# A two-layer mixture-of-experts transformer on one core: the first layer's experts in another order, the context kept on chip

## Chip, cores and metric

The kernel runs on one core of a Trainium2 chip, with fp32 inputs and outputs. The metric is the device time of one execution in microseconds, as the median of several runs. The profiler's record of one execution gives the durations and waits below; times inside it count from the start of its span.

## What is computed

512 latent tokens and 256 context tokens of width 1024 pass two layers. A layer is an attention block (three parallel head groups, one output projection) and a block of 16 experts in which each expert chooses its tokens. The second layer updates the latents alone. The change touches the expert block and the norm behind the last layer:

```python
def ec_ffn(h, router_w, w_gate, w_up, w_down):
    n_tok, d = h.shape[1], h.shape[2]
    cap = EC_CAPACITY_FACTOR * n_tok // N_EXPERTS     # 64 of 512 latents, 32 of 256 context tokens
    aff = jax.nn.softmax((h @ router_w).astype(jnp.float32), axis=-1)
    top_aff, idx = lax.top_k(jnp.swapaxes(aff, 1, 2), cap)
    xg = jax.vmap(lambda hb, ib: hb[ib])(h, idx)
    hid = jax.nn.silu(jnp.einsum('becd,edf->becf', xg, w_gate)) * jnp.einsum('becd,edf->becf', xg, w_up)
    y = jnp.einsum('becf,efd->becd', hid, w_down) * top_aff[..., None].astype(h.dtype)
    return jax.vmap(lambda yb, ib: jnp.zeros((n_tok, d), yb.dtype).at[ib.reshape(-1)].add(yb.reshape(-1, d)))(y, idx)
...
    xl = xl + g2 * ec_ffn(rmsnorm(xl, norm2_g) * (1 + sc2) + sh2, router_w, w_gate, w_up, w_down)
    if update_ctx:
        xc = xc + cg2 * ec_ffn(rmsnorm(xc, norm2_g) * (1 + csc2) + csh2, router_w, w_gate, w_up, w_down)
...
    return rmsnorm(xl, final_norm_g)
```

## The kernel before

**Streams and names.** `li` is the layer, `upd` is true in layer 0. Stream `r = 0` is the latents (four blocks of 128 tokens, `xl`), `r = 1` the context (two blocks, `xc`). Weights come from DRAM in slots of 1 MB; an expert has six (gate and up by `load_gu`, down by `load_d`, issued on SyncE's queue, `Q`). Layer 0 has 14 slots in its ring, layer 1 has 18. `S` is ScalarE (ACT), `V` VectorE (DVE), `G` GpSimd (POOL).

**Choice.** After the output projection (`wo_half`) each block is routed (`route_half`): its logits, its softmax `lg`, its normalised rows `xn` written to the DRAM table `tabx` by a DMA that GpSimd issues, and its part of `affT` (`place`, the third of the `steps`). `Choice.rounds` finds the largest entries of each expert, eight at a time, and `Choice.finish` merges two halves into the list `lt`, transposes it on TensorE and leaves the token numbers in `gidx` (rows 0 to 63 latents, 64 to 95 context).

**Experts.** `gather(e)` fetches an expert's rows from `tabx` into `xg`, which has one buffer, by an indirect DMA of GpSimd. `columns(e)` transposes them in eight TensorE operations through the PSUM tile `tp`; ACT (latents) and DVE (context) scale them into `xgT`. `gate_up(e, r)` multiplies them with the gate and up weights: latents in a tile 64 tokens wide with 512 columns, context in one 32 wide with 256. ACT takes the silu, DVE the product (`gh`). `hid_t(e, r)` transposes that and ACT copies it to `hTe`; `down(e, r)` multiplies with the down weights. In layer 1 two experts share one gather of 128 rows and one `columns`.

**Results.** In layer 0 the experts 0 to 11 (`in_dram = 12`) write `ya`, which an indirect DMA of GpSimd adds to rows of a DRAM table `acc` (one per stream); before, `acc` gets a copy of `xl` and `xc`, and later the sums are loaded back. The other experts stay on chip: the result is split into two parts of reduced mantissa (`yt`, `yp`; for four context experts together `split`, `yc`), a 0/1 matrix `pl` (`places`, on GpSimd) puts the rows back by matmuls into a PSUM tile `cb` with two buffers, and DVE adds `cb` to `xl` or `xc` half a block at a time (`combine`, a list `todo` of pieces; `fill(n)` issues n of them between other work).

**Order.** TensorE runs in the order in which the code is written. The other engines' orders come from a scheduler, before the run, and are fixed. The loop over experts is, in the order of TensorE (layer 0; layer 1 has no `r = 1`): `gate_up(e,0)`, `hid_t(e-1,·)`, some pieces, `columns(e+1)`, `gate_up(e,1)`, some pieces, `down(e-1,·)`. The reload of `xl` and `xc` from `acc` is issued on GpSimd at expert 13, ahead of the last gather in GpSimd's queue.

Of the kernel before, what the change touches and what calls it, by code (L numbers as in the profile page):

```python
# [9 lines left out]
F32 = mybir.dt.float32  # L10
# [9 lines left out]
D = 1024  # L20
# [24 lines left out]
def hybrid_kernel(ctx: ExitStack, tc: tile.TileContext, a, out):  # L45
# [108 lines left out]
    accs = [dram.tile([n, D], F32, name=f"acc{n}") for n in (NL, NCX)]  # L154
# [85 lines left out]
    def layer(li, ada):  # L240
# [535 lines left out]

        es_r = ExitStack()
# [11 lines left out]
        for r, grp in enumerate(streams):  # L789
            t = rt.tile([48, len(grp) * 64], F32, name=f"affT{r}")  # L790
            G.memset(t, 0.0)
            aff.append(t)
# [8 lines left out]
        def split_wo(hf, blk):  # L801
            o = [wop.tile([128, 512], F32R, name=f"wo{j}") for j in range(2)]
            parts(wraw[hf, blk // 4][:, blk % 4], o, S.copy)
            wo[blk] = o

        def wo_half(tb, hf, before=None, after=None, fill=()):
# [3 lines left out]
            for blk in range(8):  # L810
# [3 lines left out]
                wa, wb = wo[blk]  # L814
# [16 lines left out]
        def route_half(tb, hf):  # L831
# [12 lines left out]
            def logits():  # L844
# [19 lines left out]
                if upd:  # L864
                    i = tb - CB if tb >= CB else tb
                    G.dma_start(accs[r][i * 128:(i + 1) * 128, :], x)
# [17 lines left out]
        class Choice:  # L884


            def __init__(self, r):
                self.r, self.c = r, 0
                self.val = rt.tile([48, caps[r]], F32, name=f"val{r}")
                self.idx = rt.tile([48, caps[r]], U32, name=f"idx{r}")  # L890
                self.a = [aff[r], rt.tile([48, 4 * caps[r]], F32, name=f"affb{r}")]
# [15 lines left out]
            def finish(self):  # L907
                r, cap, np_ = self.r, caps[self.r], nparts[self.r]
                rows = 128 // np_
                v0, v1 = self.val[0:NE], rt.tile([NE, cap], F32, name="mgv")  # L910
                V.tensor_copy(v1, self.val[32:48, ::-1])
                lt = rt.tile([NE, 2, 128], F32, name="lt")
                i0, i1, ge = [rt.tile([NE, cap], F32, name=f"mg{i}") for i in range(3)]
# [30 lines left out]
                if upd:  # L944
# [12 lines left out]
        if not upd:  # L957
            load_gu(1)
        steps = []
        for hf in range(2):  # L960
            for n, tb in enumerate(tbs):
                last = n == len(tbs) - 1
                wo_half(tb, hf, (lambda blk: split_wo(0, blk)) if hf + n == 0 else None,
                        (lambda blk: split_wo(1, blk)) if hf == 0 and last else None, steps)
                steps = route_half(tb, hf)
                if hf and tb < CB:
# [16 lines left out]
        es_r.close()  # L983

# [14 lines left out]
        xgs, xgTs = {}, {}  # L999

        def gather(e):
# [306 lines left out]
```

## Time and profile before

| | |
|---|---|
| median of three runs | 1456.85 us (1455.22 to 1459.57) |
| the profiled execution | 1453.06 us, span 1451.3 us |
| TensorE, matmul | 1280.1 us busy (88% of the span) |
| VectorE / ScalarE / GpSimd | 687.3 / 517.6 / 242.2 us busy |
| mean granted TensorE clock | 0.953 of full speed |
| DMA, whole run | 321.14 MB, mean 221 GB/s |
| first expert's first matmul, layer 0 / layer 1 | 524.13 / 1204.79 us |

The time is set by chains that pass from engine to engine. TensorE is busy in most of the span, so the places that matter are those where it waits, and the length of the repeated pieces. A granted clock of 1.00 is 2.4 GHz; stretches under it had TensorE at 1.2 GHz for a part.

### The profile page before, as it was taken

Reading aid. Unit: us, or ns where it says so; the run is one execution under the profiler, and the core shown is the slowest. Engines: PE = TensorE matmul, PEld = TensorE weight load, DVE = VectorE, ACT = ScalarE, POOL = GpSimd, SP = SyncE. Lnnn points to the kernel's source line nnn. Section 1 sums busy time; section 2 is a strip of 40 time slices with the busy share of each in tenths; the row PEclk is TensorE's granted clock in tenths of the full one; section 3 lists DMA queues with packets and bytes.
Section 4 is the critical chain, followed back from the end, with each engine's and each line's share of the span. In section 5 each row is a group of like instructions: output and inputs, shape, how many; then the busy total and the mean of one; then the engine's idle time right before and its main releaser. Section 6 shows DMA issues by size and latency. Waiting matters only on the chain. (4 is left out here: it accounts for less than half of the span.)

```text
span 1451.3 us, 21505 instructions
## 1 busy us (share of the span) xinstructions
PE 1280.1 (88%) x8542; PEld 800.0 (55%) x8542; DVE 687.3 (47%) x1516; ACT 517.6 (36%) x1095; POOL 242.2 (17%) x266
## 2 busy tenths in 40 slices
PE   3989989999999869999996969998999958999994
PEld 0768866666678624444443438876777843343331
DVE  1545356566743632222222474847776351333435
ACT  2523145455533322222222143436666322232222
POOL 1111001212210222222221020102232011111203
PEclk9989999999999979999998969999999978999998
DMA  8523315444732489999999310110012857999991
GB/s 355 187 99 116 149 63 215 175 182 182 291 145 82 190 314 361 367 373 370 373 371 399 133 56 32 71 62 1 1 41 70 341 222 308 419 418 420 419 416 62
DMA packets 56195, 321.14 MB, mean 221 GB/s; under 512 B 8720, under 2 KB 10384, under 8 KB 22560
## 3 DMA queue, kind: packets, MB, share of 16 engines
q1 hardware_dynamic: 45664, 286.75, 50.7%
q0 software_dynamic: 10432, 33.04, 7.3%
q8 instruction: 67, 1.10, 0.3%
q14 instruction: 32, 0.26, 0.1%
HBM read 304.52 MB, written 15.24 MB: 220 GB/s over the span
## 5 line engine op out<-in xcount | busy, mean ns | idle before, releaser
L59 PE MATMUL mm<-slot,xgT 128*64 128x512 f32 (+1 forms) x2048 | 290.6, 493 | 0.8 <-DMA slot<-in_exp_w_up_dram 0.7
L59 PE MATMUL mm<-hT,w 128*128 128x512 f32 (+1 forms) x1176 | 230.8, 356 | 3.0 <-POOL w L140 2.0
L59 PEld LDWEIGHTS mm<-hT,w 128*128 128x128 f32 x1176 | 192.6, 192 | 37.5 <-POOL w L140 2.4
L59 PEld LDWEIGHTS mm<-slot,xgT 128*64 128x64 f32 (+1 forms) x2048 | 104.8, 125 | 170.5 <-issue 143.8
L59 PE MATMUL mm<-slot,hTe 128*32 128x256 f32 (+1 forms) x1024 | 146.8, 490 | 0.8 <-ACT hTe L1057 0.8
L1048 DVE TENSOR_TENSOR gh<-mm,gh 64x512 f32<-64x512 f32 (+1 forms) x48 | 29.0, 604 | 218.4 <-ACT gh L1047 218.4
L1047 ACT ACTIVATE gh<-mm 64x512 f32<-64x512 f32 (+1 forms) x48 | 24.9, 518 | 278.1 <-PE tp L1055 171.8
L59 PE MATMUL mm<-wo,mixb 128*128 128x512 f32 x360 | 98.2, 409 | 2.3 <-DVE mixb L140 1.4
L59 PEld LDWEIGHTS mm<-slot,hTe 128*32 128x32 f32 (+1 forms) x1024 | 48.9, 123 | 88.7 <-issue 71.3
L694 ACT COPY pt<-tp 128x512 f32<-128x512 f32 (+1 forms) x120 | 64.9, 542 | 81.3 <-PE tp L691 80.2
L691 PE MATMUL tp<-ident,p 128*128 128x128 f32 x552 | 87.1, 283 | 5.5 <-ACT pt L694 2.3
L1023 ACT ACTIVATE xgT<-tp,modT,a 128x64 f32<-128x64 f32 (+1 forms) x192 | 70.1, 425 | 58.7 <-PE tp L1019 54.3
L681 POOL TENSOR_SCALAR p<-p,sm 128x768 f32<-128x768 f32 (+1 forms) x30 | 58.5, 1951 | 124.3 <-DVE sm L680 116.0
L691 PEld LDWEIGHTS tp<-ident,p 128*128 128x128 f32 x552 | 61.1, 142 | 27.1 <-issue 18.0
L59 PEld LDWEIGHTS mm<-wo,mixb 128*128 128x128 f32 x360 | 65.1, 191 | 16.2 <-DVE mixb L140 2.2
L59 PE MATMUL ada<-slot,sT 128*32 128x512 f32 x384 | 53.7, 678 | 22.9 <-DMA slot<-in_ada_w_dram 22.9
L59 PE MATMUL sc<-kt,qh 96*128 96x512 f32 (+1 forms) x324 | 69.7, 348 | 0.0
L139 ACT CAST w<-slot 128x1024 fp32r<-128x1024 f32 x30 | 31.4, 1046 | 100.1 <-PE mm L59 73.8
L59 PE MATMUL sc<-kst,qst 128*128 128x256 f32 (+1 forms) x288 | 48.2, 298 | 20.5 <-DVE mx L678 12.7
L670 DVE TENSOR_REDUCE mx<-sc 128x1 f32<-128x768 f32 (+1 forms) x60 | 51.0, 851 | 26.9 <-PE sc L59 25.9
L59 PE MATMUL cb<-yp,pl 128*128 128x512 f32 x160 | 53.1, 449 | 11.5 <-DVE xl L1118 9.2
L1101 POOL TENSOR_SCALAR pl<-tok,st 128x512 fp32r<-128x512 f32 (+1 forms) x21 | 32.9, 1575 | 171.9 <-PE cb L59 171.8
(246 smaller groups left out, 1772.9 us busy)
## 6 DMA issues: line engine op xcount, KB each, us to landing
slot<-in_exp_w_gate_dram SPq DMA_DIRECT2D x62, 1024.0 KB
slot<-in_exp_w_up_dram SPq DMA_DIRECT2D x62, 1024.0 KB
slot<-in_exp_w_down_dram SPq DMA_DIRECT2D x62, 1024.0 KB
slot<-in_ada_w_dram SPq DMA_DIRECT2D x48, 1024.0 KB
slot<-in_win_dram SPq DMA_DIRECT2D x14, 1024.0 KB
slot<-in_wo_dram SPq DMA_DIRECT2D x8, 1024.0 KB
tabx<-xn POOLq DMA_DIRECT2D x10, 512.0 KB
xt<-in_x_dram SPq DMA_DIRECT2D x4, 512.0 KB
```

Of the source, the lines that this page charges most:

```text
L59: PE.matmul(o, l, r, start=start, stop=stop, skip_group_check=True)
L139: (hi or V.tensor_copy)(out[0], x)
L670: V.tensor_reduce(mx, sc[:, :n], axis=AX.X, op=OP.max, negate=True)
L681: (G if s and self.kind == "mla" else V).tensor_scalar(p[:, :n], p[:, :n], sm, None, op0=OP.mult)
L691: PE.transpose(ps[:, b * 128:(b + 1) * 128], p[:, (b0 + b) * 128:(b0 + b + 1) * 128], ident)
L694: S.copy(o, ps[:, :n * 128])
L1023: S.activation(xgT[:, k0 + k, :n], ps[:, k * ng:k * ng + n], AF.Identity, bias=b[:, 0:1], scale=s[:, 0:1])
L1047: S.activation(gh[64:128, :n], ps[0:64, :n], AF.Silu)
L1048: V.tensor_tensor(gh[0:64, :n], ps[64:128, :n], gh[64:128, :n], op=OP.mult)
L1101: G.tensor_scalar(pl, tok[:, :nt], slots[r][:, g:g + 1], None, op0=OP.is_equal)
```

## The change

The context's choice is put behind the first expert's latents in layer 0: the latents' choice is made at a higher priority, 64 rows are gathered, transposed and multiplied, then the context's choice runs and the gather is made again with 96 rows. In the loop, matmuls on narrow tiles are brought together (`gate_up(e,1)`, `gate_up(e,0)`, `down(e-1,0)`, `columns(e+1)`, `hid_t(e,1)`, `hid_t(e,0)`, pieces, `down(e-1,1)`); the same loop serves layer 1, where an expert's `hid_t` now follows in its own turn and the pieces come four in a row. The context's results stay on chip for all 16 experts, in four groups of four instead of one. The reload of `xl` stands one expert later, behind a small copy that reads the last `xgT`. The final norm is on VectorE for all four blocks.

```diff
-    accs = [dram.tile([n, D], F32, name=f"acc{n}") for n in (NL, NCX)]
+    accs = [dram.tile([NL, D], F32, name="acc")]
...
-                if upd:
-                    i = tb - CB if tb >= CB else tb
-                    G.dma_start(accs[r][i * 128:(i + 1) * 128, :], x)
+                if upd and tb >= CB:
+                    G.dma_start(accs[0][row:row + 128, :], x)
...
-                if hf and tb < CB:
+        for n, (hf, tb) in enumerate(order):
+            wo_half(tb, hf, (lambda blk: split_wo(0, blk)) if n == 0 else None,
+                    (lambda blk: split_wo(1, blk)) if n == len(tbs) - 1 else None, steps)
+            steps = route_half(tb, hf)
+            if tb < CB and hf:
+                with tc.high_priority(200):
                     ch[0].rounds(4)
...
         steps[0]()
         steps[1]()
         if upd:
+            with tc.high_priority(200):
+                ch[0].finish()
+        steps[2]()
+        if not upd:
+            ch[0].rounds(8)
             ch[0].finish()
-            steps[2]()
-            ch[1].rounds(4)
-        else:
-            steps[2]()
-            ch[0].rounds(8)
-        ch[-1].finish()
         es_r.close()
...
+        nall = ng
...
+        def gather(e, rows=None):
...
-            xg = xgs[e] = ex.tile([ng, D], F32, name="xg", bufs=1)
+            if e not in xgs:
+                xgs[e] = ex.tile([ng, D], F32, name="xg", bufs=1)
             c = e if upd else e // 2
-            G.indirect_dma_start(out=xg, out_offset=None, in_=tabx[li],
-                                 in_offset=bass.IndirectOffsetOnAxis(ap=gidx[:ng, c:c + 1], axis=0))
-
-        def columns(e):
+            rows = rows or slice(0, ng)
+            G.indirect_dma_start(out=xgs[e][rows], out_offset=None, in_=tabx[li],
+                                 in_offset=bass.IndirectOffsetOnAxis(ap=gidx[rows, c:c + 1], axis=0))
+
...
+        def columns(e, parts_of=(0, 1)):
...
-            xg = xgs[e]
-            xgT = xgTs[e] = ex.tile([128, KD, ng], F32, name="xgT")
+            if e not in xgTs:
+                xgTs[e] = ex.tile([128, KD, nall], F32, name="xgT")
+            xgT = xgTs[e]
+            ng = nall if 1 in parts_of else CAPL
+            xg = xgs[e][:ng]
...
-                    S.activation(xgT[:, k0 + k, :n], ps[:, k * ng:k * ng + n], AF.Identity, bias=b[:, 0:1], scale=s[:, 0:1])
-                    if upd:
+                    if 0 in parts_of:
+                        S.activation(xgT[:, k0 + k, :n], ps[:, k * ng:k * ng + n], AF.Identity, bias=b[:, 0:1], scale=s[:, 0:1])
+                    if upd and 1 in parts_of:
                         V.tensor_scalar(xgT[:, k0 + k, n:], ps[:, k * ng + n:(k + 1) * ng], s[:, 1:2], b[:, 1:2],
                                         op0=OP.mult, op1=OP.add)
...
-            if e < in_dram:
+            if r == 0 and e < in_dram:
...
-        def finish(e):
-            for r in rs:
-                down(e, r)
-                if e < in_dram:
-                    continue
-                if r == 0:
-                    pair.append((places(0, e), [Y[0][:, hf] for hf in range(2)]))
-                    if e % 2:
-                        todo.extend(combine(0, pair[-2:]))
-                elif e % 4 == 3:
-                    todo.extend(combine(1, split(e // 4)))
+        def finish(e, r):
+            down(e, r)
+            if r == 0 and e >= in_dram:
+                pair.append((places(0, e), [Y[0][:, hf] for hf in range(2)]))
+                if e % 2:
+                    todo.extend(combine(0, pair[-2:]))
+            elif r == 1 and e % 4 == 3:
+                todo.extend(combine(1, split(e // 4)))
...
-                if tb % 2:
-                    V.scalar_tensor_tensor(x, x, rs[:, 0:1], fg, op0=OP.mult, op1=OP.mult)
-                else:
-                    S.activation(x, x, AF.Identity, scale=rs[:, 0:1])
-                    G.tensor_tensor(x, x, fg, op=OP.mult)
+                V.scalar_tensor_tensor(x, x, rs[:, 0:1], fg, op0=OP.mult, op1=OP.mult)
...
-        gather(0)
-        columns(0)
+        if upd:
+
+            gather(0, slice(0, CAPL))
+            columns(0, (0,))
+            gate_up(0, 0)
+            ch[1].rounds(4)
+            ch[1].finish()
+            gather(0)
+            columns(0, (1,))
+        else:
+            gather(0)
+            columns(0)
         gather(1)
         for e in range(NE + 1):
             if e + 1 < NE and e + 1 not in wgus:
                 load_gu(e + 1, G if upd and e == 1 else Q)
+            ready = len(todo)
             if e < NE:
                 if e not in wds:
                     load_d(e, Q if upd or e > 1 else G)
-                gate_up(e, 0)
+                for r in reversed(rs):
+                    if (e, r) not in hids:
+                        gate_up(e, r)
             if e:
-                for r in rs:
-                    hid_t(e - 1, r)
-                fill(3 if upd else 2)
+                finish(e - 1, 0)
             if e < NE:
                 if e + 1 < NE:
                     columns(e + 1)
                 if e + 2 < NE:
                     gather(e + 2)
-                if upd and e == NE - 3:
-
-                    for x, acc in ((X["xl"], accs[0]), (X["xc"], accs[1])):
-                        for i, t in enumerate(x):
-                            G.dma_start(t, acc[i * 128:(i + 1) * 128, :])
-                if upd:
-                    gate_up(e, 1)
-            if e:
-                fill(3 if upd else 2)
-                finish(e - 1)
+                if upd and e == NE - 2:
+
+                    for i, t in enumerate(X["xl"]):
+                        V.tensor_copy(t[:, 0:1], xgTs[NE - 1][:, 0, 0:1])
+                        G.dma_start(t, accs[0][i * 128:(i + 1) * 128, :])
+                for r in reversed(rs):
+                    hid_t(e, r)
+            fill(min(ready, 4 if not upd else 2 if e < NE - 2 else 6))
+            if e and upd:
+                finish(e - 1, 1)
```

The order of TensorE's instructions around the first expert of layer 0. `lt` is a stream's list, `lg` a block's softmax, `xg` the gathered rows; 64x512 are the latents' matmuls and 32x256 the context's. Before:

```order
L59 MATMUL lg<-wr_3897,xT 128x16 x4
L928 MATMUL tp<-ident,lt 128x16 x2
L873 MATMUL tp<-ident,lg 16x128
L928 MATMUL tp<-ident,lt 128x16 x2
L1019 MATMUL tp<-ident,xg 128x96 x8
L59 MATMUL mm<-slot,xgT 64x512 x16
L1019 MATMUL tp<-ident,xg 128x96 x8
L59 MATMUL mm<-slot,xgT 32x256 x32
L59 MATMUL mm<-slot,xgT 64x512 x16
L1055 MATMUL tp<-ident,gh 128x64 x6
```

and with the change:

```order
L59 MATMUL lg<-wr_3899,xT 128x16 x4
L929 MATMUL tp<-ident,lt 128x16 x2
L874 MATMUL tp<-ident,lg 16x128
L1027 MATMUL tp<-ident,xg 128x64 x8
L59 MATMUL mm<-slot,xgT 64x512 x16
L929 MATMUL tp<-ident,lt 128x16 x2
L1027 MATMUL tp<-ident,xg 128x96 x8
L59 MATMUL mm<-slot,xgT 32x256 x32
L1027 MATMUL tp<-ident,xg 128x96 x8
L1064 MATMUL tp<-ident,gh 128x64 x6
L59 MATMUL mm<-slot,xgT 32x256 x32
L59 MATMUL mm<-slot,xgT 64x512 x16
```

Eight transposes of 64 rows and the latents' matmuls of expert 0 now stand between the two transposes of lists; expert 0 is transposed again with 96 rows behind the second one.

VectorE in the middle of layer 1's experts, where `xl <- xl, cb` are the additions of combined pieces and `yt`, `yp` the split of a result. Before:

```order
L1080 SCALAR_TENSOR_TENSOR yt<-mm,gw_10239,g2l 128x512
L1085 TENSOR_TENSOR yp<-yt,yp 64x512 x2
L1048 TENSOR_TENSOR gh<-mm,gh 64x512
L1118 TENSOR_TENSOR xl_3849<-xl_3849,cb 128x512 x2
L1118 TENSOR_TENSOR xl_3850<-xl_3850,cb 128x512 x2
L1080 SCALAR_TENSOR_TENSOR yt<-mm,gw_10239,g2l 128x512
```

and with the change, two experts, the first with `columns` in its turn:

```order
L1089 SCALAR_TENSOR_TENSOR yt<-mm,gw_10335,g2l 128x512
L1094 TENSOR_TENSOR yp<-yt,yp 64x512 x2
L1127 TENSOR_TENSOR xl_3846<-xl_3846,cb 128x512 x2
L1127 TENSOR_TENSOR xl_3847<-xl_3847,cb 128x512 x2
L1057 TENSOR_TENSOR gh<-mm,gh 64x512
L1089 SCALAR_TENSOR_TENSOR yt<-mm,gw_10335,g2l 128x512
L1127 TENSOR_TENSOR xl_3848<-xl_3848,cb 128x512 x2
L1127 TENSOR_TENSOR xl_3849<-xl_3849,cb 128x512 x2
L1094 TENSOR_TENSOR yp<-yt,yp 64x512 x2
L1057 TENSOR_TENSOR gh<-mm,gh 64x512
```

Before, an expert's additions follow its split and its `gh`. With the change, in one expert of two all four come behind the two `yp` of the same turn, and in the other all come ahead of them.

ScalarE with the change, at the turn of expert 13 in layer 0 (`gh` the silu, `hTe` the copies of the transposed hidden values, 128x128 the context's and 128x256 the latents'):

```order
L1056 ACTIVATE gh<-mm 64x256
L1056 ACTIVATE gh<-mm 64x512
L1032 ACTIVATE xgT<-tp,modT_110,a_0_2049 128x64 x2
L1093 CAST yp<-yt 64x512 x2
L1032 ACTIVATE xgT<-tp,modT_110,a_0_2049 128x64 x2
L1066 COPY hTe_6763<-tp 128x128
L1032 ACTIVATE xgT<-tp,modT_110,a_0_2049 128x64 x2
L1066 COPY hTe_6770<-tp 128x256
```

Two casts of the split of expert 12 stand among the scalings, ahead of the context's `hTe`; before, both copies to `hTe` stood ahead of them.

## Rows read from the trace of the kernel before

**Rows 1.** Windows of 20 us: busy us of PE, PEld, DVE, ACT, POOL; PEclk; DMA share; GB/s.

```profile
660.00:680.00 20.00, 19.47 (x170) 7.92 (x166) 4.80 (x12) 4.33 (x12) 4.05 (x3) 1.00 1.03 361
...
1300.00:1320.00 20.00, 19.30 (x92) 7.91 (x92) 8.56 (x13) 5.38 (x13) 4.12 (x3) 1.00 1.01 421
```

**Rows 2.** Waits of SyncE's DMA queue, 490 to 860: us in total, times, longest.

```profile
SPq L766 <- PE mm L59: 136.3, 25, 40.1
```

**Rows 3.** Timelines by engine, 505 to 540: start, duration, engine, line, tile, [idle before <-releaser].

```profile
505.70 0.57 POOL L863 DMA_DIRECT2D tabx<-xn  x1 [1.48 <-ACT xn L861]
...
510.14 0.17 DVE L937 CAST gidx<-tp 64x16 int32<-64x16 f32 x1 [0.55 <-PE tp L928]
...
516.33 0.17 DVE L931 TENSOR_SCALAR gidx<-tp 32x16 int32<-32x16 f32 x1 [0.54 <-PE tp L928]
...
516.78 1.02 POOL L1006 DMA_INDIRECT xg<-tabx,gidx  x1 [9.39 <-DVE gidx L931]
...
524.13 8.70 PE L59 MATMUL mm<-slot,xgT 128*64 128x512 f32 x32
...
537.16 0.20 PEld L59 LDWEIGHTS mm<-slot,xgT 128*64 128x64 f32 x4 [0.41 <-issue]
```

**Rows 4.** Timeline of PE, one expert of layer 0, 645 to 665.

```profile
645.96 7.09 PE L59 MATMUL mm<-slot,xgT 128*64 128x512 f32 x32
...
652.97 0.58 PE L1055 MATMUL tp<-ident,gh 64*128 64x64 f32 x6
...
654.57 0.55 PE L1019 MATMUL tp<-ident,xg 96*128 96x96 f32 x4 [0.53 <-ACT hTe L1057]
...
664.09 1.50 PE L59 MATMUL mm<-slot,xgT 128*64 128x512 f32 x5
```

**Rows 5.** Timeline of PEld in the same expert, where the tile's width changes.

```profile
652.02 0.14 PEld L59 LDWEIGHTS mm<-slot,xgT 128*64 128x64 f32 x2 [0.28 <-issue]
...
652.97 0.45 PEld L1055 LDWEIGHTS tp<-ident,gh 64*128 64x128 f32 x6 [0.81 <-issue]
```

**Rows 6.** Timelines of POOL and PE, last experts of layer 0, 768 to 828.

```profile
768.02 0.97 POOL L1006 DMA_INDIRECT xg<-tabx,gidx  x1 [0.30 <-issue]
...
772.89 8.48 PE L59 MATMUL mm<-slot,xgT 128*64 128x512 f32 x32
...
792.75 1.54 PE L1019 MATMUL tp<-ident,xg 96*128 96x96 f32 x8 [10.87 <-DMA xg<-tabx,gidx]
...
804.63 7.09 PE L59 MATMUL mm<-slot,xgT 128*64 128x512 f32 x32
...
826.98 1.19 PE L59 MATMUL cb<-yp,pl 128*128 128x512 f32 x4
```

**Rows 7.** Timelines of PE, DVE and ACT, one expert of layer 1, 1306 to 1324.

```profile
1306.12 7.04 PE L59 MATMUL mm<-slot,xgT 128*64 128x512 f32 x32
...
1315.38 1.33 PE L59 MATMUL cb<-yp,pl 128*128 128x512 f32 x4 [0.70 <-DVE xl L1118]
...
1316.64 3.65 PE L59 MATMUL mm<-slot,hTe 128*64 128x512 f32 x16
...
1320.13 4.46 PE L59 MATMUL mm<-slot,xgT 128*64 128x512 f32 x20
...
1307.78 1.40 DVE L1085 TENSOR_TENSOR yp<-yt,yp 64x512 fp32r<-64x512 f32 x2 [0.68 <-ACT yp L1084]
...
1314.64 1.29 DVE L1118 TENSOR_TENSOR xl<-xl,cb 128x512 f32<-128x512 f32 x2
...
1307.13 1.26 ACT L1084 CAST yp<-yt 64x512 fp32r<-64x512 f32 x2 [3.03 <-DVE yt L1080]
```

**Rows 8.** Timelines of DVE and POOL, final norm, 1435 to 1442.

```profile
1435.60 3.35 DVE L1156 SCALAR_TENSOR_TENSOR xl<-xl,rs_r,xg 128x1024 f32<-128x1024 f32 x1
...
1435.53 2.34 POOL L1159 TENSOR_TENSOR xl<-xl,xg 128x1024 f32<-128x1024 f32 x1
...
1440.40 1.28 DVE L1156 SCALAR_TENSOR_TENSOR xl<-xl,rs_r,xg 128x1024 f32<-128x1024 f32 x1 [0.93 <-POOL rs_r L147]
```

More of the change, by code (lines that the diff above doesn't have):

```diff
@@ L775, in load_d @@
                 wd += [t[:, 0], t[:, 1]]
+        es_c = ExitStack()
+        rc = pool(es_c, f"rc{li}", side="right")
         es_r = ExitStack()
@@ L789, in layer @@
         for r, grp in enumerate(streams):
-            t = rt.tile([48, len(grp) * 64], F32, name=f"affT{r}")
+            t = rc.tile([48, len(grp) * 64], F32, name=f"affT{r}")
             G.memset(t, 0.0)
@@ L888, in __init__ @@
                 self.r, self.c = r, 0
-                self.val = rt.tile([48, caps[r]], F32, name=f"val{r}")
-                self.idx = rt.tile([48, caps[r]], U32, name=f"idx{r}")
-                self.a = [aff[r], rt.tile([48, 4 * caps[r]], F32, name=f"affb{r}")]
+                self.val = rc.tile([48, caps[r]], F32, name=f"val{r}")
+                self.idx = rc.tile([48, caps[r]], U32, name=f"idx{r}")
+                self.a = [aff[r], rc.tile([48, 4 * caps[r]], F32, name=f"affb{r}")]
             def rounds(self, n):
@@ L909, in finish @@
                 rows = 128 // np_
-                v0, v1 = self.val[0:NE], rt.tile([NE, cap], F32, name="mgv")
+                v0, v1 = self.val[0:NE], rc.tile([NE, cap], F32, name="mgv")
                 V.tensor_copy(v1, self.val[32:48, ::-1])
-                lt = rt.tile([NE, 2, 128], F32, name="lt")
-                i0, i1, ge = [rt.tile([NE, cap], F32, name=f"mg{i}") for i in range(3)]
+                lt = rc.tile([NE, 2, 128], F32, name="lt")
+                i0, i1, ge = [rc.tile([NE, cap], F32, name=f"mg{i}") for i in range(3)]
                 def wide(x):
@@ L943, in finish @@
                 slots.append(st)
-                if upd:
+                if upd and r == 0:
                     pi = mods.tile([128, NE], I32, name=f"pi{r}")
@@ L958, in layer @@
             load_gu(1)
+        order = [(hf, tb) for hf in range(2) for tb in tbs]
         steps = []
[L960 to L965, printed above, removed]
-                if hf and tb < CB:
+        for n, (hf, tb) in enumerate(order):
[4 more added lines that the diff above has]
+                with tc.high_priority(200):
                     ch[0].rounds(4)
@@ L975, in layer @@
         if upd:
-            ch[0].finish()
-            steps[2]()
-            ch[1].rounds(4)
-        else:
-            steps[2]()
-            ch[0].rounds(8)
-        ch[-1].finish()
+            with tc.high_priority(200):
[3 more added lines that the diff above has]
+            ch[0].rounds(8)
+            ch[0].finish()
         es_r.close()
+        if not upd:
+            es_c.close()
         esp.close()
@@ L1204, in layer @@
         es_x.close()
+        if upd:
+            es_c.close()
         es_b.close()
```

6 lines of the change are left out of this document (2 added, 4 removed).

## The prediction

> **What bounds the kernel now.** I read the windows first, then the timeline of one expert in each layer, then the places where TensorE waits. In a window of layer 0's experts TensorE is busy 19.47 of 20 us at the full clock, and in one of layer 1's 19.30 [rows 1]. DMA stands at a share of 1.03 and 1.01 there, so the windows alone don't say which of the two sets the pace. The waits of SyncE do: its weight loads wait 25 times, 136.3 us in all, for matmuls to give a slot back [rows 2]. Weights are ahead of their use; TensorE sets the pace. An expert of layer 0 takes 18.13 us from `gate_up` to `gate_up` (645.96 to 664.09), with one wait inside, 0.53 us for ACT's copy to `hTe` [rows 4]. One of layer 1 takes 14.01 (1306.12 to 1320.13) with a wait of 0.70 for DVE's additions [rows 7]. Two places of layer 0 are not steady: the start, where one chain of choice, gather and transposes holds the first matmul until 524.13 [rows 3], and expert 15's rows, for which TensorE idles 10.87 us [rows 6]. The sum below is made on the profiled execution, 1453.06 us, which lies 3.8 under the median 1456.85; I add it to the median.
>
> **Start of layer 0.** Before, the latents' `gidx` was ready at 510.14 and the context's at 516.33, and one gather at 516.78 gave the first matmul at 524.13, 7.35 later [rows 3]. The new first gather needs the latents' numbers alone, so at most 6.2 us could be won. It also needs the whole `tabx`. The last block's row went out at 505.70 [rows 3]; now the latents' choice has the higher priority on DVE, that block's softmax sinks behind it, and with it the write: I put the gather at 513.3 (512 to 514.5). For 64 rows I take 6.9 of the 7.35, which gives the first matmul at 520.2, and 8.6 for `gate_up(0,0)` at its old length: 528.8. But the order shows the context's two list transposes behind that `gate_up` on TensorE. So the choice of the context is hidden, and its end is not: transposes, `gidx`, 1.1 us, then the second gather with transposes, then, since `xg` has one buffer, the gather of expert 1 behind that. Transposes take less where TensorE has not idled just before (0.55 for four against 1.54 for eight behind the long wait, [rows 4, 6]), so I take 6.3 for each: 529.9, 536.2, 542.5 for expert 1's first matmuls. Before, these stood at 537.16 [rows 3]. TensorE has done 0.6 us of hidden transposes more by then. **+4.7**, with +3 to +7 for gathers of 5.5 to 7.35. The first expert starts some 4 us earlier and the second 5 later.
>
> **Width order, 13 steady experts of layer 0.** Two changes of the tile's width go per expert. On PEld a load behind one had 0.81 us of idle time where others had 0.28 [rows 5], so a change costs at most 0.53; on PE the next matmul starts where the last one's modelled end is (645.96 + 7.09 against 652.97, [rows 4]), which speaks for little, and I take 0.16 for each: −0.3. The copy for the context's `hTe` now stands behind a scaling on ACT, and the latents' `hid_t` waits for its PSUM buffer about 0.9 instead of 0.53 [rows 4]: +0.4. **+1** over 13 experts, −10 if a change is worth the full 0.53.
>
> The Trainium skill (TensorEngine Tiling (Array Packing), Key Properties) says that a change of tiling mode drains TensorE. By it the width order would be a real gain; the 0.81 on the load side agrees in direction, and the size is taken from the rows alone.
>
> **The context on chip.** Gone are two copies to DRAM, twelve scatter-additions and the reload of `xc`, none of which TensorE waits for by itself. New are three groups of four pieces with two matmuls each. Four such matmuls take 1.12 us (826.98 to 828.10 by the duration 1.19 less its overlap, [rows 6]), so a piece costs 0.56, twelve cost **+6.7**. The DVE additions, 0.65 each [rows 7], and the split lie beside 18 us experts; if they didn't, a piece would cost about 0.1 more.
>
> **Last experts of layer 0.** The reload stood ahead of the gather of expert 15 on GpSimd: issued at 768.02, its rows released TensorE at 792.75. Expert 14's turn took 31.74 us (772.89 to 804.63, [rows 6]) against 18.13: 13.6 lost, the idle 10.87, a wait for weights (8.48 against 7.09) and matmuls at the lower clock behind the idle time. The reload now comes after all gathers: **−13.7** (−15 to −9, should weights still be late or the reload be in the way of the tail). In its place ACT's two casts of `yp` (1.26, [rows 7]) stand ahead of the context's `hTe` at experts 13 and 14, as the order shows. They need the end of `down` and `yt`, so the latents' `hid_t` waits some 2 us twice: **+4.1**. The last additions end where they did by my addition of pieces: six `fill`s take the place of two threes. Layer 0 in all: 4.7 + 1 + 6.7 − 13.7 + 4.1 = **+2.8**, and by my estimate 1.4 off for waits for DVE among the last pieces, which the longer fill shortens: +1.4 (±5).
>
> **Layer 1.** The same loop puts `down(e-1)`, `columns`, `hid_t(e)` and four pieces in a row. In the six experts that have `columns` the order shows DVE's additions behind the split of the same turn. After `down` the split takes until 1307.78 + 1.40, which is 3.06 behind 1306.12 [rows 7]. `cb` has two buffers, so the third piece waits for the first addition: 3.06 + 0.65 + about 0.1 behind `down`, the fourth 0.65 later, and then the piece itself: 5.2 behind `down`. With 6.97 for `gate_up` and 3.50 for `down` [rows 7] that is 15.7 for the turn instead of 14.0: +1.7, six times, **+10.3**. In the six without `columns` additions come first, and the wait of 0.70 goes down to 0.3: **−2.3**. The start: `hid_t(0)` comes right behind `gate_up(0)` and waits for silu and product, +1.7; a wait of one copy goes: **+1.6**. The final norm: a product of 128x1024 on DVE took 3.35 beside GpSimd's 2.34 and 1.28 alone [rows 8]. Without GpSimd's two the last block is ready 2 to 4 us earlier: **−3.0** (−5 to 0). Layer 1: **+6.5** (±2 unless the stall isn't there, below).
>
> **Sum.** +1.4 + 6.5 = +7.9: 1461.0 on the profiled execution, 1464.7 against the median; I say 1464.
>
> **Rivals.**
> *Memory paces layer 0* (faster, 0.15). The DMA share of 1.03 at 361 GB/s has no gap [rows 1], and TensorE did wait for expert 14's weights [rows 6]. If transfers set the 18.13, the twelve scatter-additions, worth about 0.8 us of transfer each (128 KB, read and written back, beside 6.3 MB of weights per 18.13 us), would give back 10 to 12, and the pieces would lie in waiting time: 1464 − 12 − 6.7 = 1445. Against it: SyncE's 136.3 us of waiting for slots [rows 2], and one idle place per expert, released by ACT [rows 4].
> The Trainium skill (DMA: Bandwidth & Descriptors, Specifications) gives about 358 GB/s of HBM for one core, by which layer 0's 361 would be at the limit. The 421 GB/s in layer 1 [rows 1] contradict it here, so the rival keeps its small chance.
> *Layer 1's additions don't stall* (no change, 0.22). Where the fourth piece slides into time that TensorE loses anyway, or DVE gets to the additions before the casts, 8 to 10 us of the 10.3 go: about 1455. For it: before, the same four pieces cost 0.70 of waiting. Against it: DVE's order is fixed and stands in the rows of the order.
> *Width changes cost what PEld shows* (0.10). 16 experts by two by 0.35 more than I took: −11, about 1453.
> *The start goes worse* (slower, 0.05). If the second gather takes as long as expert 15's, which stood behind other transfers, its weights being queued in front: +6 more, 1470.
> *My sum* (0.48). From the five: faster 0.20 (the first, half of the third), within 0.3% 0.30, slower 0.50. A measurement of this kernel tells about 0.3%, 4.4 us. The range goes from 1448, which leaves out the strongest form of memory's pace, to 1474, which is the sum with the start, the reload and the final norm at their bad ends.
>
> **What the profile should show.** Layer 0's first matmul near 520 and expert 1's near 542; turns of 18.2; no idle 11 us at expert 15, but two of about 2 us on the latents' `hid_t` at experts 13 and 14, released by ACT. In layer 1, turns that alternate between about 15.7 and 13.6, with waits for DVE's `xl` in the longer ones; DVE's last products of 1.28. Wrong would be: turns of layer 0 under 17.9 (memory or widths), even turns of 14 in layer 1, or an expert 1 that starts before 538.

## The result and the profile after

The changed kernel took 1470.65 us (median of six runs, 1465.14 to 1471.22) against 1456.03 for the kernel before (six runs, 1453.12 to 1461.04): a ratio of 1.0091, 95% interval 1.0074 to 1.0108. Eight more runs, taken with experiments below, gave 1466.44, ratio 1.0069 (1.0041 to 1.0097). So it is slower, by 0.7 to 0.9%; the forecast was 1464, slower, in 1448 to 1474.

The span of the profiled execution grew from 1451.3 to 1469.0 us. Where, is read from starts on TensorE's timeline. To take out what happened before the change's reach, I count layer 0 from the start of the last output matmuls ahead of the first choice (`mm<-wo,mixa`, at 498.25 before and 502.20 after), and layer 1 from its first expert matmul to the end of the span:

| us | before | after | difference |
|---|---|---|---|
| first expert matmul | 25.9 | 25.4 | −0.5 |
| expert 2's | 57.0 | 67.2 | +10.2 |
| expert 13's | 256.5 | 266.3 | +9.8 |
| expert 14's | 274.6 | 289.7 | +15.1 |
| expert 15's | 306.4 | 313.4 | +7.0 |
| layer 1's first transposes | 354.4 | 362.2 | +7.8 |
| length of layer 1's experts | 246.5 | 250.9 | +4.4 |

The stretches that are left differ by 5.6 us in these two executions, 4.0 of it ahead of the count, where the granted clock is 1.00 in one and 0.96 in the other between 400 and 490 us. I take that for chance: the count starts at 498.25, 500.53 and 502.83 in three kernels whose edits all come later (before, and experiments 4 and 9 below). 12 us is what the traces give to the change.

The windows after, as in [rows 1], from a stretch of each layer's experts (busy us of PE, PEld, DVE, ACT, POOL; clock; DMA share; GB/s):

```profile
580.00:600.00 20.00, 19.61 (x172) 8.39 (x170) 6.93 (x16) 4.66 (x13) 2.51 (x2) 1.00 1.02 392
...
1290.00:1310.00 20.00, 18.44 (x88) 7.51 (x84) 7.49 (x12) 5.35 (x13) 1.01 (x1) 1.00 1.01 418
```

Layer 0 is as full as before; in layer 1 TensorE has lost 0.9 us in 20. The waits of TensorE between 510 and 862 (us in total, times, longest):

```profile
PE tp L1027 <- DMA xg<-tabx,gidx: 16.1, 2, 11.1
PE tp L1064 <- ACT hTe L1066: 9.5, 15, 2.3
PE cb L59 <- DVE yp L1094: 3.5, 1, 3.5
```

The 10.87 us of [rows 6] are gone, as foretold: the two waits for `xg` in the first row are those of the start. Fifteen waits for ACT's copy to `hTe` add up to 9.5, two of them 2.3 long.

The start of layer 0 after, which answers to [rows 3] (timelines of POOL, DVE and PE):

```profile
513.22 0.57 POOL L865 DMA_DIRECT2D tabx<-xn  x1 [1.48 <-ACT xn L863]
...
521.88 1.00 POOL L1011 DMA_INDIRECT xg<-tabx,gidx  x1 [6.96 <-issue]
...
513.03 0.17 DVE L938 CAST gidx<-tp 64x16 int32<-64x16 f32 x1
...
537.58 0.17 DVE L932 TENSOR_SCALAR gidx<-tp 32x16 int32<-32x16 f32 x1 [17.02 <-PE tp L929]
...
538.03 1.03 POOL L1011 DMA_INDIRECT xg<-tabx,gidx  x1 [10.35 <-DVE gidx L932]
...
526.45 1.08 PE L1027 MATMUL tp<-ident,xg 64*128 64x64 f32 x8 [11.06 <-DMA xg<-tabx,gidx]
527.60 9.72 PE L59 MATMUL mm<-slot,xgT 128*64 128x512 f32 x32
...
542.58 1.54 PE L1027 MATMUL tp<-ident,xg 96*128 96x96 f32 x8 [5.04 <-DMA xg<-tabx,gidx]
...
551.01 5.34 PE L59 MATMUL mm<-slot,xgT 128*32 128x256 f32 x68
```

The latents' numbers were ready at 513.03. The last rows of the table were sent at 513.22, and the profile's list of transfers (513 to 523) gives the time from issue to landing:

```profile
tabx<-xn POOLq DMA_DIRECT2D x1, 512.0 KB, 7.8
```

The gather left at 521.88, when they had landed. Behind it everything stands in one chain, as the order had shown: the first expert, the context's `gidx`, a second gather (5.04 us of waiting), its transposes, a third, and expert 1 at 551.01.

A steady turn after, to be held against [rows 4] (timeline of PE):

```profile
569.39 10.65 PE L59 MATMUL mm<-slot,xgT 128*32 128x256 f32 x96
...
584.94 0.46 PE L1064 MATMUL tp<-ident,gh 64*128 64x64 f32 x4 [0.39 <-ACT hTe L1066]
...
587.08 10.65 PE L59 MATMUL mm<-slot,xgT 128*32 128x256 f32 x96
```

17.69 us instead of 18.13, with a wait of 0.39 instead of 0.53. Expert 13's turn, and the clock in windows ahead of and behind its wait:

```profile
782.47 0.88 PE L1027 MATMUL tp<-ident,xg 96*128 96x96 f32 x8
...
785.87 0.68 PE L1064 MATMUL tp<-ident,gh 64*128 64x64 f32 x4 [2.26 <-ACT hTe L1066]
786.48 2.07 PE L59 MATMUL cb<-yc,pl 128*128 128x512 f32 x4
788.48 3.64 PE L59 MATMUL mm<-slot,hTe 128*32 128x256 f32 x32
791.90 10.87 PE L59 MATMUL mm<-slot,xgT 128*32 128x256 f32 x96
```

```profile
768.00:783.00 15.00, 15.00 (x130) 6.14 (x123) 5.42 (x11) 2.57 (x5) 0.76 (x1) 1.00 1.03 378
786.00:792.00 6.00, 6.00 (x44) 3.20 (x48) 2.54 (x8) 1.67 (x5) 0.00 (x0) 0.50 1.01 341
```

TensorE waits 2.26 us for ACT's copy, which stands behind the two casts (ACT):

```profile
783.69 1.24 ACT L1093 CAST yp<-yt 64x512 fp32r<-64x512 f32 x2
...
785.55 0.26 ACT L1066 COPY hTe<-tp 128x128 f32<-128x128 f32 x1
```

What follows runs at half the clock (0.50 granted, 1.2 GHz, against 1.00): four `cb` matmuls take 2.07 instead of 1.2, the context's `down` 3.64 instead of 1.93. The turn takes 23.45 us.

Layer 1, to be held against [rows 7] (timelines of PE and DVE):

```profile
1281.60 7.09 PE L59 MATMUL mm<-slot,xgT 128*64 128x512 f32 x32
...
1295.92 1.33 PE L59 MATMUL cb<-yp,pl 128*128 128x512 f32 x4 [1.25 <-DVE xl L1127]
1297.18 7.09 PE L59 MATMUL mm<-slot,xgT 128*64 128x512 f32 x32
...
1309.53 1.33 PE L59 MATMUL cb<-yp,pl 128*128 128x512 f32 x4 [0.31 <-DVE xl L1127]
1310.79 1.51 PE L59 MATMUL mm<-slot,xgT 128*64 128x512 f32 x6
...
1292.17 0.75 DVE L1089 SCALAR_TENSOR_TENSOR yt<-mm,gw,g2l 128x512 f32<-128x512 f32 x1 [2.04 <-PE mm L59]
1293.74 1.41 DVE L1094 TENSOR_TENSOR yp<-yt,yp 64x512 fp32r<-64x512 f32 x2 [0.82 <-ACT yp L1093]
1295.18 1.29 DVE L1127 TENSOR_TENSOR xl<-xl,cb 128x512 f32<-128x512 f32 x2
```

Turns of 15.58 and 13.61 alternate; in the long one the third piece waits 1.25 us for an addition that starts behind both `yp`. Before, `columns` stood between the two pairs of pieces and filled that time (1.03 us of transposes from 1300.56 in the trace before). The last products of the final norm, to be held against [rows 8]:

```profile
1459.77 2.48 DVE L1161 SCALAR_TENSOR_TENSOR xl<-xl,rs_r,xg 128x1024 f32<-128x1024 f32 x2
...
1463.17 1.28 DVE L1161 SCALAR_TENSOR_TENSOR xl<-xl,rs_r,xg 128x1024 f32<-128x1024 f32 x1 [0.66 <-POOL rs_r L147]
```

1.24 to 1.28 each, none near 3.35.

### The profile page after: what moved, and what is told of

It reads as the page before. It is cut to its first block, busy times and chain, and to the rows that moved or that the text cites. A ratio compares the mean times of both kernels' runs of the same rounds, so it can differ in the third digit from the quotient of the medians.

```text
span 1469.0 us, 21577 instructions
## 1 busy us (share of the span) xinstructions
PE 1297.8 (88%) x8574; PEld 816.7 (56%) x8574; DVE 716.3 (49%) x1572; ACT 514.0 (35%) x1096; POOL 223.0 (15%) x252
## 5 line engine op out<-in xcount | busy, mean ns | idle before, releaser
L59 PE MATMUL mm<-slot,xgT 128*32 128x256 f32 (+1 forms) x2048 | 291.2, 497 | 0.7 <-ACT xgT L1032 0.3
L59 PEld LDWEIGHTS mm<-slot,xgT 128*32 128x32 f32 (+1 forms) x2048 | 105.1, 126 | 168.3 <-issue 135.9
L1056 ACT ACTIVATE gh<-mm 64x512 f32<-64x512 f32 (+1 forms) x48 | 24.8, 517 | 270.3 <-PE mm L59 270.3
L59 PEld LDWEIGHTS mm<-slot,hTe 128*32 128x32 f32 (+1 forms) x1024 | 52.5, 127 | 86.7 <-issue 77.5
L691 PEld LDWEIGHTS tp<-ident,p 128*128 128x128 f32 x552 | 61.3, 142 | 27.1 <-issue 18.8
L1011 POOL DMA_INDIRECT xg<-tabx,gidx x25 | 24.3, 972 | 314.9 <-PE tp L1064 196.7
L59 PE MATMUL cb<-yp,pl 128*128 128x512 f32 x160 | 55.3, 465 | 17.5 <-DVE xl L1127 10.7
L59 PE MATMUL sc<-kst,qst 128*128 128x256 f32 (+1 forms) x288 | 48.8, 301 | 20.7 <-DVE mx L678 13.0
L670 DVE TENSOR_REDUCE mx<-sc 128x1 f32<-128x768 f32 (+1 forms) x60 | 51.0, 850 | 26.6 <-PE sc L59 25.7
```

The source lines that it names most:

```text
L59: PE.matmul(o, l, r, start=start, stop=stop, skip_group_check=True)
L670: V.tensor_reduce(mx, sc[:, :n], axis=AX.X, op=OP.max, negate=True)
L691: PE.transpose(ps[:, b * 128:(b + 1) * 128], p[:, (b0 + b) * 128:(b0 + b + 1) * 128], ident)
L1011: G.indirect_dma_start(out=xgs[e][rows], out_offset=None, in_=tabx[li], in_offset=bass.IndirectOffsetOnAxis(ap=gidx[rows, c:c + 1], axis=0))
L1056: S.activation(gh[64:128, :n], ps[0:64, :n], AF.Silu)
```

## Experiments

Ten kernels ran. The table gives each one's median with the median of the kernel before from the same set of runs, and its trace counted as above.

| kernel | us (before) | first | expert 2 | expert 13 | expert 15 | layer 0's end | layer 1 |
|---|---|---|---|---|---|---|---|
| before | | 25.9 | 57.0 | 256.5 | 306.4 | 354.4 | 246.5 |
| changed | 1470.65 (1456.03) | 25.4 | 67.2 | 266.3 | 313.4 | 362.2 | 250.9 |
| 1 old start | 1457.92 (1456.93) | 26.2 | 59.0 | 258.1 | 305.1 | 353.9 | 250.8 |
| 2 no priority | 1460.08 (1456.93) | 21.2 | 64.4 | 263.4 | 306.4 | 354.9 | 250.8 |
| 3 old layer 1 | 1458.93 (1456.93) | 24.4 | 66.0 | 265.0 | 310.9 | 359.5 | 241.6 |
| 4 before, late reload | 1441.37 (1456.93) | 25.4 | 56.8 | 256.3 | 294.1 | 342.6 | 246.2 |
| 5 changed again | 1466.44 (1455.75) | 24.8 | 65.7 | 264.9 | 311.9 | 360.7 | 250.6 |
| 6 copies first | 1454.80 (1455.75) | 24.5 | 65.8 | 264.9 | 302.9 | 352.2 | 250.6 |
| 7 context in DRAM | 1459.87 (1455.75) | 25.7 | 66.5 | 261.1 | 306.0 | 354.6 | 251.6 |
| 8 combined | 1435.65 (1455.75) | 25.3 | 58.6 | 253.1 | 291.9 | 340.7 | 242.5 |
| 9 before, late reload, norm | 1442.87 (1458.43) | 25.9 | 57.1 | 256.6 | 294.2 | 342.6 | 243.0 |
| 10 two early | 1446.79 (1458.43) | 22.7 | 61.1 | 264.8 | 302.2 | 351.3 | 243.0 |

**1. The changed kernel with the old start.**

```diff
-                with tc.high_priority(200):
-                    ch[0].rounds(4)
+                ch[0].rounds(4)
...
-            with tc.high_priority(200):
-                ch[0].finish()
+            ch[0].finish()
...
+            ch[1].rounds(4)
+            ch[1].finish()
...
-            gather(0, slice(0, CAPL))
-            columns(0, (0,))
-            gate_up(0, 0)
...
+        gather(0)
+        columns(0)
```

> The changed kernel with its start put back: both choices before the first gather, one gather of 96 rows, no raised priority; loop, context on chip, layer 1 and final norm as changed. My account: in the changed kernel the last table row leaves at 513.22 and takes 8.2 us to land, so the first gather goes at 521.88 instead of 516.78, and two more gathers stand in a chain behind it; expert 1 starts 13 us later than before. Then this kernel has its first expert matmul near 524 and expert 1's near 538, and is 12 to 14 us faster than the changed one, about 1458. Rival: the start is only shifted, and layer 0 catches up because weights are read ahead meanwhile; then 0 to 4 us.

Ratio to before 1.0007 (0.9989 to 1.0025). Its start (POOL, PE):

```profile
511.05 0.57 POOL L865 DMA_DIRECT2D tabx<-xn  x1 [1.48 <-ACT xn L863]
...
522.84 1.06 POOL L1012 DMA_INDIRECT xg<-tabx,gidx  x1 [0.99 <-DVE gidx L932]
...
529.77 12.22 PE L59 MATMUL mm<-slot,xgT 128*32 128x256 f32 x96 [0.20 <-DVE xgT L1035]
```

The table's row goes 11.8 us ahead of the gather, which waits for `gidx` alone. From there the traces run in parallel: expert 2 comes 8.2 us earlier than in the changed kernel, layer 0 ends 8.3 us earlier, layer 1 is the same. Nothing of the start's loss is caught up later, so the rival falls. The medians say 12.7, or 8.5 against the changed kernel's second set of runs. By the traces that is less than the 12 to 14 expected: the expectation compared times from the start of the span, and 4.0 of its 13 us lie ahead of the count. Against the kernel before, expert 2 still comes 2.0 later here, 0.6 of it for transposes done earlier; the rest belongs to the new loop and not to the split start.

**2. The changed kernel without the raised priority.**

```diff
-                with tc.high_priority(200):
-                    ch[0].rounds(4)
+                ch[0].rounds(4)
...
-            with tc.high_priority(200):
-                ch[0].finish()
+            ch[0].finish()
```

> The changed kernel without the two raised priorities of the latents' choice; the split of the first expert stays. My account: the last table row leaves near 505.7 again and lands near 514, the first gather goes near 514.5 instead of 521.9, so the first matmul comes near 520; the chain of list transposes, second gather and third gather behind it stays. 6 to 8 us faster than the changed kernel, about 1463. Rival: the gather waits for the queue of weight transfers and not for the table; then it stays within 2 us of 521.9 and the time within 2 us of the changed kernel.

Ratio 1.0009 (0.9981 to 1.0037).

```profile
506.16 0.57 POOL L865 DMA_DIRECT2D tabx<-xn  x1 [1.48 <-ACT xn L863]
...
514.71 1.00 POOL L1009 DMA_INDIRECT xg<-tabx,gidx  x1 [7.38 <-DVE idx L906]
...
519.86 9.34 PE L59 MATMUL mm<-slot,xgT 128*64 128x512 f32 x32
...
544.70 11.35 PE L59 MATMUL mm<-slot,xgT 128*32 128x256 f32 x96
```

The table's last rows leave at 506.16 and take 7.6 us to land; the gather leaves 8.55 us behind their issue, as it did 8.66 behind it in the changed kernel. So it waits for the table, and not for `gidx`, whose list was ready for its transposes at 510.19 here. The first matmul comes 4.7 us earlier than before the change, at 21.2; but expert 1 still starts at 46.0, for the chain behind the first expert is whole, and expert 2 at 64.4, 7.4 us later than before. Against the changed kernel the start wins 2.8, less than I expected. Layer 0 ends 7.2 earlier; 4.2 of the other 4.4 come from the turns of experts 13 and 14 (22.3 and 20.7 us), where the same waits on ACT stand. Behind the second of them the matmuls keep their short durations (PE):

```profile
801.83 0.46 PE L1062 MATMUL tp<-ident,gh 64*128 64x64 f32 x4 [2.25 <-ACT hTe L1064]
802.22 1.21 PE L59 MATMUL cb<-yc,pl 128*128 128x512 f32 x4
803.37 1.93 PE L59 MATMUL mm<-slot,hTe 128*32 128x256 f32 x32
```

So a wait of 2.25 us does not bring the clock down each time.

**3. The changed kernel with the old loop in layer 1** (a loop of its own for layer 1, as it stood before).

```diff
+                gate_up(e, 0)
+            if e:
+                hid_t(e - 1, 0)
+                fill(2)
...
+                    columns(e + 1)
...
+            if e:
+                fill(2)
+                finish(e - 1, 0)
```

> The changed kernel with layer 1's loop in the order of before (transposes of hidden values one turn later, pieces two and two around the columns); layer 0 and the final norm as changed. My account: turns of 15.58 and 13.61 us become 14.0 each, and the second expert's matmuls start 3 us earlier: 7 to 9 us faster than the changed kernel, about 1462. Rival: the additions' wait costs nothing that another wait would not take: within 2 us of the changed kernel.

Ratio 1.0017 (0.9997 to 1.0037). Two turns of it (PE):

```profile
1268.58 7.04 PE L59 MATMUL mm<-slot,xgT 128*64 128x512 f32 x32
...
1282.59 7.04 PE L59 MATMUL mm<-slot,xgT 128*64 128x512 f32 x32
```

Layer 1's experts take 241.6 us instead of 250.9, with turns of 14.0 us. The loop costs 9.3 in this pair of traces, a little more than expected.

**4. The kernel before with the reload one expert later.**

```diff
-                if upd and e == NE - 3:
+                if upd and e == NE - 2:
...
+                            V.tensor_copy(t[:, 0:1], xgTs[NE - 1][:, 0, 0:1])
                             G.dma_start(t, acc[i * 128:(i + 1) * 128, :])
```

> The kernel before with one edit: the reload of the sums one expert later, behind the last gather. My account: the idle 10.87 us at expert 15's rows goes with the slower matmuls behind it, and the rest stays: 12 to 14 us faster than before, about 1443. Rival: the loss moves to the end of layer 0, where the additions then wait for the reload, or expert 14's weights stay late: 0 to 5 us faster.

Ratio 0.9904 (0.9875 to 0.9934): 15.6 us faster. The transposes of expert 15's rows and the start of its turn (PE):

```profile
785.12 0.55 PE L1019 MATMUL tp<-ident,xg 96*128 96x96 f32 x4 [0.53 <-ACT hTe L1057]
...
794.63 7.09 PE L59 MATMUL mm<-slot,xgT 128*64 128x512 f32 x32
```

The wait of 10.87 us is gone. Expert 14's turn takes 19.7 us (274.4 to 294.1) instead of 31.8, and the end of layer 0 keeps its length (48.5, 48.0 before).

**5. The changed kernel again.**

> The changed kernel once more, unedited, beside the three below. The first six runs gave 1465 to 1471, 14.6 above before; the profiled executions, cut at the last output matmul ahead of the first choice and at layer 1's first expert, give 7.7 us for layer 0's experts and 4.4 for layer 1's, 12 in all, and the rest lies in stretches that the change leaves as they were. If that rest is the clock's chance, this gives about 1468; if it belongs to the change, 1470.6 again.

1466.44; between its two sets of runs the unedited kernel moved by 4 us. The 12 us of the traces lie between the two differences of the medians, 14.6 and 10.7.

**6. The changed kernel with the copies to `hTe` ahead of the casts.**

```diff
-            S.copy(hT, ps[:, :n // 2])
+            with tc.high_priority(60 if upd else 0):
+                S.copy(hT, ps[:, :n // 2])
```

> The changed kernel with the copies to hTe at a raised priority in layer 0, so that at experts 13 and 14 the context's copy stands ahead of the casts of yp on ScalarE. My account: the two waits of 2.26 us fall to 0.39, the matmuls behind them keep the full clock, and the two turns go from 23.4 and 23.7 us to about 19: 8 to 9 us faster than the changed kernel. Rival: only the waits go and the clock falls anyway for another reason: 3 to 4 us faster.

Ratio 0.9997 (0.9975 to 1.0019), 11.6 us under the changed kernel of the same set. Expert 13's turn (PE):

```profile
778.18 0.46 PE L1064 MATMUL tp<-ident,gh 64*128 64x64 f32 x4 [0.39 <-ACT hTe L1067]
778.57 1.20 PE L59 MATMUL cb<-yc,pl 128*128 128x512 f32 x4
779.69 1.94 PE L59 MATMUL mm<-slot,hTe 128*32 128x256 f32 x32
```

The wait is 0.39, and the pieces and the context's `down` behind it take 1.20 and 1.94, the full clock's durations. The two turns take 18.8 and 19.2 us instead of 23.5 and 23.6. Without the waits the granted clock stays at 1.00 through both (778 to 800), so they are what made it fall; by experiment 2 they don't do so each time.

**7. The changed kernel with the context in DRAM.**

```diff
-            if r == 0 and e < in_dram:
+            if e < in_dram:
...
-            elif r == 1 and e % 4 == 3:
+            elif r == 1 and e >= in_dram and e % 4 == 3:
```

(and the two copies, the places and the reload of `xc` as before, behind the last gather).

> The changed kernel with the context's results of experts 0 to 11 in DRAM again (two copies out, twelve scatter-additions, reload of xc behind the last gather); all else as changed. My account: twelve pieces of 0.56 us on TensorE go, 6.7 us faster, turns of layer 0 all 17.7. Rival, memory paces layer 0: turns get longer than 17.7 by the scatter-additions' transfers, and the gain is under 2 us or a loss.

Ratio 1.0029 (1.0013 to 1.0046), 6.6 us under the changed kernel. All turns of experts 2 to 12 take 17.7 us; a window of them:

```profile
640.00:660.00 20.00, 19.61 (x174) 8.48 (x172) 5.13 (x13) 4.45 (x13) 4.05 (x3) 1.00 1.03 366
```

The twelve scatter-additions are back, and TensorE is as full as without them. Memory does not pace layer 0's steady turns, and the pieces cost what was foretold. Near the end of the layer, though, weights come late (PE):

```profile
785.71 8.94 PE L59 MATMUL mm<-slot,xgT 128*32 128x256 f32 x60 [1.93 <-DMA slot<-in_exp_w_up_dram]
```

TensorE waits 1.93 us for expert 14's weights, and the waits on ACT at experts 13 and 14 stand as in the changed kernel. The five kernels with the context in DRAM and the late reload (4, 7, 8, 9 and 10) all wait for expert 14's weights, 0.28 to 1.93 us; the six with the context on chip don't. Why was not tested.

**8. Combined:** old start, width order in layer 0 with the copies first, context in DRAM, late reload, old loop in layer 1, norm on VectorE (the edits of 1, 3, 6 and 7 together).

> What seemed to be worth having, together: the start of before, the width order in layer 0 with the copies to hTe ahead of the casts, the context in DRAM, the reload behind the last gather, layer 1's loop of before, the final norm on VectorE. By the parts: 15.5 for the reload, 0.44 us in each of 13 turns, 4.9 for the norm, about 26 us faster than before, 1431. Rival: the gains overlap (the wait for expert 15's rows and the end of layer 0): no faster than the reload alone, 1441.

Ratio 0.9881 (0.9824 to 0.9937), 20 us under before, less than the sum. By the medians it is not settled that this is more than the reload alone, since the interval of experiment 4 lies within this one; by the traces it is, with layer 0 1.9 and layer 1 3.7 us shorter than there. Against before, layer 1 gives 4.0. In layer 0 the turns of experts 2 to 12 give 4.9 and the start takes 1.6; then expert 14's weights are late (PE):

```profile
774.09 8.94 PE L59 MATMUL mm<-slot,xgT 128*32 128x256 f32 x60 [1.61 <-DMA slot<-in_exp_w_up_dram]
```

That turn takes 21.1 us, 1.61 of it this wait, against 19.7 in experiment 4.

**9. Before with the late reload and the norm.**

```diff
-                if tb % 2:
-                    V.scalar_tensor_tensor(x, x, rs[:, 0:1], fg, op0=OP.mult, op1=OP.mult)
-                else:
-                    S.activation(x, x, AF.Identity, scale=rs[:, 0:1])
-                    G.tensor_tensor(x, x, fg, op=OP.mult)
+                V.scalar_tensor_tensor(x, x, rs[:, 0:1], fg, op0=OP.mult, op1=OP.mult)
```

> The kernel before with two edits, the reload behind the last gather and the final norm on VectorE; the loops as before in both layers. It says whether the width order earns anything in all. The reload alone gave 1441.4 and the norm is worth 4.6 to 4.9 by layer 1's length in two traces: 1436.6, the same as the combined kernel's 1435.7 within 0.3%. If the width order's 0.44 us per turn arrives in the end, the combined kernel is 5 us faster than this one.

Ratio 0.9893 (0.9866 to 0.9919): 15.6 us under before, where 20 was expected, and no more than the reload alone gave. In the traces layer 1 is 3 us shorter than in experiment 4, so the norm's gain is there; the medians, from two sets of runs, don't show it. Its layer 0 ends at 342.6 and the combined one's at 340.7, so of the width order's 0.44 us a turn 1.9 arrive; the start and the late weights of expert 14 take the rest. The ratios of the two kernels overlap: whether the combined one is the faster isn't settled.

**10. Two experts' latents early** (the combined kernel; no priority; `xg` with two buffers).

```diff
+            gather(0, lat)
+            gather(1, lat)
+            columns(0, (0,))
+            gate_up(0, 0)
+            columns(1, (0,))
+            hid_t(0, 0)
+            ch[1].rounds(4)
+            ch[1].finish()
+            gate_up(1, 0)
+            gather(0)
+            gather(1)
```

> The combined kernel with another early start: no raised priority, the latents of the first two experts gathered before the context's choice into two buffers, so that the second expert's latent matmuls cover the second gather. If the loss of the split start is the chain of gathers behind the first expert, covering it brings expert 2's first matmul from 58.6 us behind the last output matmul ahead of the choice (combined) to about 56: 2 to 3 us faster than the combined kernel, 1433. Rival: the later gathers stand behind the weights' transfers as the table's last row does, and nothing is gained or up to 3 us are lost.

Ratio 0.9918 (0.9895 to 0.9941): not faster than the combined kernel, and its layer 0 is 10.6 us longer. The second gather is covered, no wait for it is left; the waits of TensorE between 510 and 860:

```profile
PE tp L1026 <- DMA xg<-tabx,gidx: 9.0, 1, 9.0
PE mm L59 <- DMA slot<-in_exp_w_up_dram: 6.4, 5, 2.4
```

In its place weights come late five times, 6.4 us. Expert 2 starts at 61.1, not at 56, and turns of 19.5 and 24.3 us stand among those of 17.7. Why the weights fall behind (their loads are issued from another queue and in another order here) wasn't tried.

## Why the prediction came out as it did

Direction and range held: slower by 0.7 to 0.9% where 0.5% was said. The sum had +7.9 and the traces give +12.1; behind that lie errors of both signs. Term by term:

| us | foretold | measured in the traces |
|---|---|---|
| start of layer 0, at expert 2 | +4.7 | +9.6 |
| width order, 13 turns | +1 | −5.7 |
| context on chip, twelve pieces | +6.7 | +6.7 |
| reload, expert 14's turn | −13.7 | −13.6 |
| casts ahead of the copy, experts 13 and 14 | +4.1 | +9.5 |
| last pieces of layer 0 | −1.4 | +1.4 |
| layer 1's loop | +9.6 | +8.4 |
| final norm | −3.0 | −3.9 |

The start, the casts and the last pieces came out 13 us worse than foretold, the width order and layer 1 some 9 us better. That the forecast's time is near is in part luck. (The column adds up to 12.4 and not 12.1, as layer 1's two rows are means over several kernels.)

- **The start** failed most: +4.7 foretold, +9.6 measured (10.2 less 0.6 of transposes done earlier). "I put the gather at 513.3" is 15.0 behind the start of the count, and the prediction names no time for the table's last write to land; the gather came 19.7 behind that start. The write was sent at 11.0, 3.6 later than with no raised priority (7.45 before and in experiment 2), and took 7.8 to land. Experiment 2 shows nearly the same 8.55 from write to gather with the write sent early. The write was hidden before by the context's choice (505.70 to 516.78 in [rows 3]); making the choice shorter uncovered it, and the raised priority made it later. The chain behind the first gather was right: 29.1 us from there to expert 1's matmuls (521.88 to 551.01) where 29.2 was said (513.3 to 542.5).
- **Width order:** a turn is 0.44 shorter where 0.08 longer was said. A turn under 17.9 was named as a sign of being wrong, for memory or for widths; it was neither. The wait for `hTe` was wrong, 0.39 and not 0.9, and that makes up the whole difference. The price of a width change, 0.16, holds: 0.14 of the 0.44 is the shorter wait, and 0.30 is left for two changes. No run changes the widths alone; the 0.30 is what the matmuls of two turns differ by. The Trainium skill (TensorEngine Tiling (Array Packing), Key Properties) says that a change of tiling mode drains the engine. What it costs here, 0.15 us a change, is far from the 0.53 that PEld's rows [rows 5] would allow.
- **Context on chip:** +6.7 foretold. A turn with two pieces takes 18.81 against 17.69, 1.12 more; six turns have two, which makes 6.7. Experiment 7 against experiment 5 gives 6.1 by layer 0's end and 6.6 by the medians.
- **Reload:** −13.7 foretold. In the changed kernel no wait for rows or weights is left at experts 14 and 15, so all 13.6 that expert 14's turn had over a plain one are gone. In experiment 4, where the weights are still late, it is 12.1 in that turn, 11.8 by layer 0's end and 15.6 by the median. The rival that the loss moves on is out.
- **Experts 13 and 14:** the order was read rightly and the waits were 1.87 us longer than the usual ones, as said; that the clock would halve behind them was not seen. Together with the pieces the two turns cost 11.7 over two plain ones of 17.69: 2.2 for the pieces, 3.7 for the waits, and 5.8 left for the clock. Experiment 6 takes 8.5 to 9.1 of it back.
- **Last pieces:** from expert 15's start to the end of layer 0 it takes 48.8 us, against 48.0 before, although 0.6 of transposes were already done. A wait of 3.54 for `yp` on DVE stands there; before, the longest among the pieces was 2.22 for `xl`. The 1.4 that the longer fill was to save is not there. No run tests why.
- **Layer 1:** turns of 15.7 and 13.6 foretold, 15.58 and 13.61 measured; the loop costs 8.4 (250.9 against 242.5, the mean of four kernels with the old loop and the new norm) where 9.6 was said. The norm gives 3.9 (242.5 against 246.4, the mean of two with the old one) where 3.0 was said.
- **Rivals:** memory as layer 0's pace is refuted for the steady turns (experiment 7); weights came late at expert 14 in the kernels that keep the context in DRAM (before in [rows 6], 4 and 7 to 10), and in experiment 10 at other experts too. The rival that the start goes worse gave 1470, near the measured time, but for another reason: the second gather took 6.0 to the matmuls where 6.3 was said, and it was the first that came late. That additions in layer 1 would not stall is refuted by the rows.

## What to carry to other kernels

Before a stage is begun earlier, look up what else it waits for: a transfer that had been hidden by the work now cut short becomes the next bound, and its time to land counts, not its issue. A wait of 2 us on a full engine cost more than twice its length where the clock fell behind it, so the order on the engine that makes the copy is worth a look at each turn that differs from its neighbours. Parts of a change that belong to different places should be timed apart: one edit here, a reload moved behind one gather, was worth 12 us by the trace and 15.6 by the medians, and was more than eaten up by its companions.

## What was not expected of the hardware

- A write of 512 KB to `tabx` in DRAM took 7.4 to 8.2 us from issue to landing at the start of layer 0's experts (the changed kernel, experiments 1 and 2), while weight transfers filled the DMA engines (share 1.02 between 513 and 522 us); the median of the changed kernel's ten such writes is 3.0. That the weights are the cause was not tested.
- After a wait of 2.26 us at a full clock, the granted clock stood at 0.50 from 786 to 792 us; waits of 0.39 to 0.53 in the other turns left it at 1.00. The changed kernel and experiments 1, 2, 3, 5 and 7 have twelve waits of 2.25 or 2.26 us in all. Behind eleven of them matmuls take longer than at the full clock, for some 6 us or for less; behind one, in experiment 2, they don't (1.21 us for four `cb` matmuls). What decides stays open.
- Stretches that the edits leave as they were differ by up to 4.6 us between executions, which is as much as several edits here are worth. In one of them the granted clock shows it (0.96 against 1.00). Lengths counted from a start near the edit repeated far better (layer 1 of the changed loop: 250.6 to 251.6 in six kernels).
